# Order of products in the first projection, of casts in the down projection, and of one weight pair among the residual's quarters

## The chip, the core and the metric

The kernel runs on one core of a Trainium2 chip. The metric is the device time of one execution in microseconds (us), as a median over several runs. Engines are called PE (TensorE, matmuls), DVE (VectorE), ACT (ScalarE), POOL (GpSimd) and SP (SyncE, which issues most transfers). Each engine works through its own instructions in a fixed order and waits where an operand or a buffer is not ready.

## The reference

One block of a hybrid encoder on 256 tokens and 2048 channels in float32:

```python
hn = rmsnorm(h, mix_norm_pre)
proj = hn @ w_in                     # z, xbc, dt, u
y_ssd = ssd_mixer(z, xbc, dt, ...)   # two-directional scan, 16 heads
y_pool = pool_mixer(u, ...)
h = h + rmsnorm(concat(y_ssd, y_pool) @ w_out, mix_norm_post)
hn = rmsnorm(h, ffn_norm_pre)
gate, val = split(hn @ w_ffn_up)     # 2 x 5632 columns
ff = (gelu(conv(gate)) * val) @ w_ffn_down
h = h + rmsnorm(ff, ffn_norm_post)
gate = sigmoid(rmsnorm(h, ple_norm_pre) @ w_ple_gate)
h = h + rmsnorm(gate * (p @ w_ple), ple_norm_post)
```

## The kernel before

**Products.** A float32 product is made of three products of a shorter type. `split` (its ACT cast is L153, its DVE subtraction L154) turns a piece of weights, once its raw data have landed, into a high half (name ending in h) and a low half (ending in l, the source less the high half). `put` (L190 on ACT, L191 on DVE) does the same for activations. For each piece PE then multiplies high by high (`q == 0` in the code), and the two mixed products: `q == 1` uses the low weights, `q == 2` the low activations. All matmuls go through `mm` (L90). There are 3 buffers of raw weights, 5 each of high and low halves, 2 of the down projection's activations (`hs`), six PSUM banks called main and two called misc. Except in the up stage, where the order is written out, the order of each engine's instructions comes from the scheduler of the framework, which works from the order of the program, dependences and buffers.

**Stages on PE**, in order of time: dtu (the columns of the input projection that give dt and u), xbc, z, the scan and wo (output projection), up (gate and value columns), down, ple (second half) with the residual, gate, and the last norm.

**dtu.** The loop takes 16 tiles of 128 rows of `w_dtu` with 1056 columns each, and treats these as three thirds of 352 columns; for each of the two token halves t there are three thirds and three products, 18 matmuls per tile. The first tile is cast in three pieces, the second in pieces of 704 and 352 columns, all later ones whole. The tile of k is needed with its normalised inputs `hn(k)` (hnh, hnl in the trace). While the last tiles run, ACT reads the whole of x twice for the row norms (`rxj`, L404), builds operands for the scan, and casts the first weights of xbc (`xb_0h`, `xb_1h`); then ACT and DVE copy dtu's six banks out (`u`, L531 to L534, and `dt`, L530), and a small transpose `rxbp` on PE follows. The xbc matmuls use banks that these copies free.

**down.** 44 tiles of the hidden size, in 22 pairs (u from 0 to 21), for each half of the output columns (halves 0 and 1, main loop of `sublayer`). A pair in the list `dn_fast` goes through `seven_products`, which combines blocks (names dn..a, b, c, d, sums dns and hd) and needs fewer matmuls; a pair outside the list is a plain pair of `token_major` with whole weights (`dn_0h`, `dn_1h` and their low halves, raw tile `dn1r`). `get(k)` returns the activations of a tile and, at first use, makes them with `hid_split` (ACT cast L937, DVE subtraction L938, tile `hs`). Plain pairs between pairs of `dn_fast` are u = 6 in half 0 and u = 6, 10 and 17 in half 1; in the trace dn134 is that of u = 17, dn140 and dn142 are the last two pairs, which are plain too, and stand at the end of the list of tiles in half 1.

**Residual and gate.** Behind the last sum of down, the loop over four quarters c in `sublayer` adds the normed result to the residual (`hb`, L858), transposes that quarter on PE (`panel_part`, L391) and puts it as `dnxh` and `dnxl`. The gate matmuls (`gt`) of the quarters that are ready fill PE in between; their first weight pair (`gtf`, loaded early by `first`) is ready long before, the next pairs (`gt02`, `gt04`, `gt01` and so on; `gt_0h` and `gt_0l` in the trace, raw tile `gt0r`) are split as the gate loop comes to them. The second half of ple is copied out of its banks by ACT (`pl`, L869).

Of the kernel before, what the change touches and what calls it, by code (L numbers as in the profile page):

```python
# [53 lines left out]
def build(nc, a, out):  # L54
# [6 lines left out]
    with tile.TileContext(nc) as tc, \  # L61
# [27 lines left out]
        def mm(o, lhsT, rhs, start, stop):  # L89
            last["pe"] = ins(nc.tensor.matmul(o, lhsT, rhs, start=start, stop=stop, skip_group_check=True))  # L90
# [51 lines left out]
        def split(name, src, nel, cuts=()):  # L142

            if name in ready:
                return ready.pop(name)
            if name in spare:
                hi, lo = spare.pop(name)
            else:
                hi = wp.tile([P, 1056], F32R, tag="whi", bufs=5, name=f"{name}h")
                lo = wp.tile([P, 1056], F32R, tag="wlo", bufs=5, name=f"{name}l")  # L150
            for c0, c1 in zip((0, *cuts), (*cuts, nel)):
                s = slice(c0, c1)
                last["act"] = ins(nc.scalar.copy(hi[:, s], src[:, s]))  # L153
                last["dve"] = ins(nc.vector.tensor_sub(lo[:, s], src[:, s], hi[:, s].bitcast(F32)))  # L154
            return hi, lo
# [31 lines left out]
        def put(dst, src, scale):  # L187
# [3 lines left out]
                    ins(nc.vector.scalar_tensor_tensor(lo, src, scale, hi.bitcast(F32),  # L191
                                                       op0=ALU.mult, op1=ALU.subtract)))

        work = []

        chain = {}
# [108 lines left out]
        def token_major(name, w, c0, ks, get, acc, tail=1, fast=(), alt=None, sums=None, at=()):  # L305


            group, nu = [], len(ks) // 2
            for u in range(nu):
                if u in at:  # L310
                    at[u]()
                k0 = ks[2 * u]
                if u in fast:
                    if u == fast[0]:
                        alt = alt + [misc(f"{name}s{i}") for i in (2, 3)]
                    seven_products(f"{name}{k0}", name[:2], w, k0, c0, sums(k0), acc, alt, u == fast[0], u == fast[-1])
                    continue
                r = None if f"{name}{k0}_0" in ready else raw(f"{name}r{k0}", w[c0 // 1024, k0 // 2])
                for j in range(2):
                    group.append((k0 + j, *split(f"{name}{k0}_{j}", r and r[:, j * 1024:(j + 1) * 1024], 1024)))  # L320
                if nu - tail <= u < nu - 1:
                    continue

                order = [(t, o, g, q) for t in range(2) for o in columns(acc[t]) for g in group for q in range(3)] \
                    if u == nu - 1 or u - 1 in fast[-1:] else \
                    [(t, o, g, q) for g in group for t in range(2) for q in range(3) for o in columns(acc[t])]
                for t, (o, c), (k, wh, wl), q in order:
                    xh, xl = (v[:, t * P:(t + 1) * P] for v in get(k))
                    xx, ww = ((xh, wh), (xh, wl), (xl, wh))[q]
                    c = (c + 512 * (k + 1)) % 1024  # L330
                    mm(o, xx, ww[:, c:c + o.shape[-1]], k == ks[0] and q == 0, k == ks[-1] and q == 2)
                if u - 1 in fast[-1:]:
                    combine(name, acc, alt, nu - tail == u + 1 and tail > 1)
                group = []
                aside()
            if nu in at:
                at[nu]()
# [116 lines left out]
        for u in range(0, NK, 2):  # L454
            r = [wp.tile([P, 2048], F32, tag="raw", bufs=3, name=f"dtur{u}") if u else r0, page(f"dtur{u + 1}")]
            for j in range(2):
                k = u + j
                if k == 0:
                    last["dma"] = load(r[0][:, 704:1056], w_dtu[0][:, 704:1056])
                    xload(1, 2)  # L460
                    x_panel(1, 2)
                    continue
                for c0, c1 in ((0, 704), (704, 1056)) if k == 1 else ((0, 1056),):
                    last["dma"] = load(r[j][:, c0:c1], w_dtu[k][:, c0:c1])
                if k == 1:
                    xload(2, 4)
                elif k in (3, 5, 7):
                    xload(*{3: (4, 9), 5: (9, 13), 7: (13, 16)}[k])
                elif k == 4:
                    load(vt, a["columns"][:, :V_N - V_SCW])  # L470
                elif k == 6:
                    load(small, a["columns"][:, V_N - V_SCW:])
            if u:
                x_panel(u, u + 2)
            for j in range(2):
                k = u + j
                with tc.issue_after(front[0]), tc.issue_after(front[1]):
                    wh, wl = split(f"dtu{k}", r[j][:, :1056], 1056, ((352, 704), (704,))[k] if k < 2 else ())
                if k == 8:
                    half = last["act"], last["dve"]  # L480

                def part(t, q, ns=range(3)):
                    xh, xl = (v[:, t * P:(t + 1) * P] for v in hn(k))
                    xx, ww = ((xh, wh), (xh, wl), (xl, wh))[q]
                    for n in ns:
                        o = acc2[t][:, :352] if n == 2 else acc[t][n][:, :352]
                        mm(o, xx, ww[:, n * 352:(n + 1) * 352], k == 0 and q == 0, k == NK - 1 and q == 2)


                for a_ in ([(t, q, (n,)) for n in range(3) for q in (0, 2, 1) for t in range(2)] if k == 0 else  # L490
                           [(t, q) for t in range(2) for q in range(3)]):
                    part(*a_)

        with tc.issue_after(half[0]), tc.issue_after(half[1]):
# [293 lines left out]
        def gload(name, src):  # L788
            g = cp.tile([P, D], F32, tag="gain", name=name)
            load(g, src.partition_broadcast(P))  # L790
            return g
# [34 lines left out]
                return dict(self.got[k], a11=(h1[:, :P], l1[:, :P]), a12=(h2[:, :P], l2[:, :P]),  # L826
                            a22=(h2[:, P:], l2[:, P:]))

        def sublayer(name, w, ks, get, gain, h, vnext, panel=Panel, fast=((), ()), sums=None, at=(), row=None):

            mg = [page(f"{name}m{t}") for t in range(2)]
            sq = [[], []]
# [22 lines left out]
            for c in range(4):  # L855
                s = slice(c * 512, (c + 1) * 512)
                for t in range(2):
                    nc.vector.scalar_tensor_tensor(h[t][:, s], mg[t][:, s], r[t], h[t][:, s],  # L858
                                                   op0=ALU.mult, op1=ALU.add)
                panel_part(f"{name}x", pan, h, vnext, 4 * c, 4 * c + 4)  # L860
            return pan

        def ple(half):
# [219 lines left out]
        def first():  # L1083
# [3 lines left out]
            for j in range(2):  # L1087
                c = slice(j * 1024, (j + 1) * 1024)
                spare[f"gt00_{j}"] = hi[:, c], lo[:, c]
                ready[f"gt00_{j}"] = split(f"gt00_{j}", r[:, c], 1024)  # L1090

        hp = sublayer("dn", w_down, list(range(NF)), hid_get, gload("gffn", a["ffn_norm_post"][0]), h, V_PN,
                      fast=dn_fast, sums=hid_sums, at={11: first, NF // 2: lambda: (ple_parts(), back())}, row=rf)


        pl = [page("plb")]
# [154 lines left out]
```

## Time and profile before

| what | value |
|---|---|
| runs | 1116.56, 1115.88 and 1116.61 us, median 1116.56 |
| the profiled execution's own time | 1116.13 us |
| its span | 1114.4 us |
| granted TensorE clock | 0.998 |
| stages on PE (us from the span's start) | dtu 4.7 to 52.1, xbc to 141, z to 197, wo to 290, up to 786, down to 1009, residual and ple to 1026, gate to 1105 |

The profile is that of one execution. Its rows give a start, a duration, the engine, the line, the operation, and the tiles in the form output<-inputs with a number of instructions; in brackets stands how long the engine was idle before it, and what ended the idle time. A row of the timeline can hold several equal instructions in a row, and tile names are printed without their numbers, so that `dn_0h` stands for each plain pair's. A PE matmul is drawn longer than it keeps PE from the next one, since matmuls overlap; so distances between starts tell its cost.

### The profile page before, as it was taken

To read this page: it belongs to the slowest core of one execution; us is meant where nothing else is said; L and a number is where in the kernel's file an instruction comes from. 1 tells how busy PE (TensorE), PEld (TensorE's weight loads), DVE (VectorE), ACT (ScalarE), POOL (GpSimd) and SP (SyncE) were. 2 spreads that over 40 slices of the span, in tenths; PEclk is the share of its full clock that TensorE was granted. 3 is DMA by queue.
4 is the path that set the end of the run, shared out by engine and by line. 5 is a ranking of instruction groups with operands and counts; after the bars stand their busy time and mean duration, and the time that the engine had idled before them with its cause. 6 is when DMAs were issued, how large, how long until landed. Compare 5 with 4: busy or idle time off the path is not lost.

```text
span 1114.4 us, 16061 instructions
## 1 busy us (share of the span) xinstructions
PE 1104.0 (99%) x5964; PEld 950.6 (85%) x5964; DVE 959.6 (86%) x1338; ACT 723.8 (65%) x1056; POOL 69.0 (6%) x140
## 2 busy tenths in 40 slices
PE   9999999999999999999999999999999999999997
PEld 9999988888888888888888888888888888877876
DVE  6568997899868998888888888888899999989895
ACT  6858763555775565664655655657689878767673
POOL 0200000100100000000000000000000000001001
PEclk9999999999999999999999999999999999999999
DMA  9753346454589999999899999999999899995662
GB/s 363 314 204 137 117 188 263 151 189 178 195 343 397 382 396 385 361 378 374 335 378 385 356 377 366 352 393 391 362 382 381 322 348 403 415 378 222 265 235 105
DMA packets 54943, 347.29 MB, mean 312 GB/s; under 512 B 6096, under 2 KB 6992, under 8 KB 20176
## 3 DMA queue, kind: packets, MB, share of 16 engines
q1 hardware_dynamic: 44064, 289.53, 66.8%
q0 software_dynamic: 10368, 56.10, 13.3%
q8 instruction: 47, 0.77, 0.3%
q10 hardware_dynamic: 432, 0.62, 0.2%
q14 instruction: 32, 0.26, 0.1%
HBM read 297.48 MB, written 48.76 MB: 311 GB/s over the span
## 4 chain that ended last, share of the span: by engine, by line
PE 94%; DVE 2%; ACT 2%; issue 1%; POOL 1%; DMA 0%; SPq 0%; POOLq 0%; ACTq 0%
PE ga L90 22%; PE va L90 22%; PE dna L90 12%; PE woa L90 7%; PE xbc L90 5%; PE gt L90 5%; PE z L90 4%; PE dns L90 4%; PE dtu L90 4%; PE dn0s L90 2%; PE dn1s L90 2%; PE yd L90 1%; PE pw L90 1%; PE gts L90 1%; PE ple L90 1%
## 5 line engine op out<-in xcount | busy, mean ns | idle before, releaser
L90 PE MATMUL ga<-wox,ug_0h 128*128 128x512 f32 x352 | 125.5, 395 | 0.0
L90 PE MATMUL ga<-wox,ug_1h 128*128 128x512 f32 x352 | 125.1, 394 | 0.0
L90 PE MATMUL va<-wox,uv_1h 128*128 128x512 f32 x352 | 124.8, 393 | 0.0
L90 PE MATMUL va<-wox,uv_0h 128*128 128x512 f32 x352 | 124.8, 393 | 0.0
L90 PE MATMUL ga<-wox,ug_1l 128*128 128x256 f32 x352 | 99.1, 282 | 0.0
L90 PE MATMUL va<-wox,uv_1l 128*128 128x256 f32 x352 | 99.1, 281 | 0.0
L90 PE MATMUL va<-wox,uv_0l 128*128 128x256 f32 x352 | 99.1, 281 | 0.0
L90 PE MATMUL ga<-wox,ug_0l 128*128 128x256 f32 x352 | 99.0, 281 | 0.0
L253 DVE TENSOR_TENSOR dnb<-dnb 128x512 f32<-128x512 f32 x128 | 88.3, 690 | 3.1
L90 PEld LDWEIGHTS va<-wox,uv_1h 128*128 128x128 f32 x352 | 66.1, 188 | 15.0
L90 PEld LDWEIGHTS ga<-wox,ug_1h 128*128 128x128 f32 x352 | 66.1, 188 | 15.0
L90 PEld LDWEIGHTS va<-wox,uv_0h 128*128 128x128 f32 x352 | 66.1, 188 | 15.0
L90 PEld LDWEIGHTS ga<-wox,ug_0h 128*128 128x128 f32 x352 | 66.1, 188 | 14.9
L90 PEld LDWEIGHTS ga<-wox,ug_0l 128*128 128x128 f32 x352 | 66.2, 188 | 0.1
L90 PEld LDWEIGHTS ga<-wox,ug_1l 128*128 128x128 f32 x352 | 66.2, 188 | 0.0
L90 PEld LDWEIGHTS va<-wox,uv_0l 128*128 128x128 f32 x352 | 66.2, 188 | 0.0
L90 PEld LDWEIGHTS va<-wox,uv_1l 128*128 128x128 f32 x352 | 66.2, 188 | 0.0
L937 ACT CAST hs<-hid 128x512 fp32r<-128x512 f32 x44 | 27.3, 621 | 21.8 <-PE dna L90 21.6
L244 POOL DMA_DIRECT2D dns<-dnb x30 | 16.2, 541 | 310.9 <-DVE dnb L253 310.9
L938 DVE TENSOR_TENSOR hs<-hid,hs 128x512 fp32r<-128x512 f32 x44 | 30.2, 686 | 5.8 <-ACT hs L937 5.8
L801 ACT CAST he<-he 128x512 fp32r<-128x512 f32 x13 | 8.1, 621 | 37.7 <-DVE he L800 37.7
L90 PE MATMUL dna<-dn_1h,hs 128*128 128x512 f32 x96 | 30.9, 393 | 0.0
(2247 smaller groups left out, 3227.7 us busy)
## 6 DMA issues: line engine op xcount, KB each, us to landing
dnb<-w_down SPq DMA_DIRECT2D x32, 1024.0 KB, 9.8
dns<-dnb POOLq DMA_DIRECT2D x30, 1024.0 KB, 6.6
hd<-hsum POOLq DMA_DIRECT2D x24, 512.0 KB, 8.3
zr<-w_z SPq DMA_DIRECT2D x8, 1024.0 KB, 4.9
dtur<-w_dtu SPq DMA_DIRECT2D x14, 528.0 KB, 8.6
wo0r<-w_out_ SPq DMA_DIRECT2D x7, 1024.0 KB, 4.9
dn1r<-w_down SPq DMA_DIRECT2D x7, 1024.0 KB, 6.8
hsum<-he POOLq DMA_DIRECT2D x13, 512.0 KB, 7.7
```

The lines of the kernel that those rows point to most:

```text
L90: last["pe"] = ins(nc.tensor.matmul(o, lhsT, rhs, start=start, stop=stop, skip_group_check=True))
L244: nc.gpsimd.dma_start(t, pg[0])
L253: nc.vector.tensor_add(v[:, i], v[:, i], v[:, j])
L801: nc.scalar.copy(o[:, :512], s[:, :512])
L937: nc.scalar.copy(t[:, :512], hid_part(k))
L938: nc.vector.tensor_sub(t[:, 512:], hid_part(k), t[:, :512].bitcast(F32))
```

## The change

It has three parts.

1. In dtu the order of the products of a tile is changed. The first tile keeps its order. In the second and third, for each third of the columns, both tokens' products with high weights come first, and then all products with the low weights. In tiles 3 to 13 both tokens' high-weight products come before the low-weight ones, and in the last two tiles each token half has its low-weight product last. The stop flag of the last tile moves to the product that now comes last. The third tile's weights are cast and subtracted in two pieces, of 352 and 704 columns. No matmul is added or removed.
2. In `token_major` a plain pair that stands between two pairs of the list `fast` calls `get(k0)` directly after the pair's weight splits, ordered behind the pair's last ACT cast (`issue_after`). In down this holds for u = 6 of half 0 and u = 6, 10 and 17 of half 1. In wo `get` only returns slices, and gate has no such pair.
3. `sublayer` takes a dictionary `then` of functions to be called behind the quarters of the residual. In down's call, the function `second` loads and splits the two pieces of gate's second weight pair (`gt02`) there, one behind quarter 1 and one behind quarter 2; the gate loop then finds them in `ready`.

In the built program the changes of order are local. In dtu DVE and ACT have one more instruction each. At the border to xbc the first bank's u copies are spread otherwise over ACT and DVE, so that xbc's first bank is freed by a DVE copy of u (and by ACT's cast `xb_0h`), and its second by an ACT copy. The activations of the four plain pairs stand behind the weights' casts on ACT. On DVE, the last two pairs' low halves of weights stand ahead of sums of the banks, and `gt02`'s first low half stands between the first and second pair of the first quarter's `dnxl`, ahead of the residual's third quarter, its second low half ahead of the fourth. On PE five matmuls of `gt02` stand ahead of the third quarter's transposes, and four more gate matmuls ahead of `gt01`'s first ones. On SP one load (`plb`) stands behind a load of gate weights where it stood ahead of it; POOL's order is the same.

```diff
--- before.py
+++ after.py
@@ -191,6 +191,7 @@
                     ins(nc.vector.scalar_tensor_tensor(lo, src, scale, hi.bitcast(F32),
                                                        op0=ALU.mult, op1=ALU.subtract)))
 
+        LOW_LAST = (0, 2), (1,)
         work = []
 
         chain = {}
@@ -320,6 +321,9 @@
                     group.append((k0 + j, *split(f"{name}{k0}_{j}", r and r[:, j * 1024:(j + 1) * 1024], 1024)))
                 if nu - tail <= u < nu - 1:
                     continue
+                if fast and fast[0] < u < fast[-1]:
+                    with tc.issue_after(last["act"]):
+                        get(k0)
 
                 order = [(t, o, g, q) for t in range(2) for o in columns(acc[t]) for g in group for q in range(3)] \
                     if u == nu - 1 or u - 1 in fast[-1:] else \
@@ -475,7 +479,7 @@
             for j in range(2):
                 k = u + j
                 with tc.issue_after(front[0]), tc.issue_after(front[1]):
-                    wh, wl = split(f"dtu{k}", r[j][:, :1056], 1056, ((352, 704), (704,))[k] if k < 2 else ())
+                    wh, wl = split(f"dtu{k}", r[j][:, :1056], 1056, ((352, 704), (704,), (352,))[k] if k < 3 else ())
                 if k == 8:
                     half = last["act"], last["dve"]
 
@@ -484,11 +488,13 @@
                     xx, ww = ((xh, wh), (xh, wl), (xl, wh))[q]
                     for n in ns:
                         o = acc2[t][:, :352] if n == 2 else acc[t][n][:, :352]
-                        mm(o, xx, ww[:, n * 352:(n + 1) * 352], k == 0 and q == 0, k == NK - 1 and q == 2)
+                        mm(o, xx, ww[:, n * 352:(n + 1) * 352], k == 0 and q == 0, k == NK - 1 and q == 1)
 
 
                 for a_ in ([(t, q, (n,)) for n in range(3) for q in (0, 2, 1) for t in range(2)] if k == 0 else
-                           [(t, q) for t in range(2) for q in range(3)]):
+                           [(t, q, (n,)) for qs in LOW_LAST for n in range(3) for q in qs for t in range(2)] if k < 3 else
+                           [(t, q) for t in range(2) for q in (0, 2, 1)] if k > NK - 3 else
+                           [(t, q) for qs in LOW_LAST for t in range(2) for q in qs]):
                     part(*a_)
 
         with tc.issue_after(half[0]), tc.issue_after(half[1]):
@@ -826,7 +832,7 @@
                 return dict(self.got[k], a11=(h1[:, :P], l1[:, :P]), a12=(h2[:, :P], l2[:, :P]),
                             a22=(h2[:, P:], l2[:, P:]))
 
-        def sublayer(name, w, ks, get, gain, h, vnext, panel=Panel, fast=((), ()), sums=None, at=(), row=None):
+        def sublayer(name, w, ks, get, gain, h, vnext, panel=Panel, fast=((), ()), sums=None, at=(), row=None, then=()):
 
             mg = [page(f"{name}m{t}") for t in range(2)]
             sq = [[], []]
@@ -858,6 +864,8 @@
                     nc.vector.scalar_tensor_tensor(h[t][:, s], mg[t][:, s], r[t], h[t][:, s],
                                                    op0=ALU.mult, op1=ALU.add)
                 panel_part(f"{name}x", pan, h, vnext, 4 * c, 4 * c + 4)
+                if c in then:
+                    then[c]()
             return pan
 
         def ple(half):
@@ -1089,8 +1097,13 @@
                 spare[f"gt00_{j}"] = hi[:, c], lo[:, c]
                 ready[f"gt00_{j}"] = split(f"gt00_{j}", r[:, c], 1024)
 
+        def second(j):
+            if j == 0:
+                cur["gt"] = raw("gt0r2", w_gate[0, 1])
+            ready[f"gt02_{j}"] = split(f"gt02_{j}", cur["gt"][:, j * 1024:(j + 1) * 1024], 1024)
+
         hp = sublayer("dn", w_down, list(range(NF)), hid_get, gload("gffn", a["ffn_norm_post"][0]), h, V_PN,
-                      fast=dn_fast, sums=hid_sums, at={11: first, NF // 2: lambda: (ple_parts(), back())}, row=rf)
+                      fast=dn_fast, sums=hid_sums, at={11: first, NF // 2: lambda: (ple_parts(), back())}, row=rf, then={1: lambda: second(0), 2: lambda: second(1)})
 
 
         pl = [page("plb")]
```

## The prediction

> **What bounds the kernel now.** I read the busy line first, then the table of TensorE's (PE's) waits, then PE's timeline at the places which the change touches, and last the engine that releases each wait there.
>
> ```profile
> PE 1104.0 (99%) x5964; PEld 950.6 (85%) x5964; DVE 959.6 (86%) x1338; ACT 723.8 (65%) x1056; POOL 69.0 (6%) x140
> ```
>
> PE works for 1104.0 of 1114.4 us, so nearly all of the time is matmul work, and the change takes no matmul away. Only time in which PE stands or crawls can be won. The waits that the table names at the places of the change are small:
>
> ```profile
> PE gt L90 <- DVE gt_0l L154: 0.8, 1, 0.8
> ...
> PE dna L90 <- ACT dn_0h L153: 0.3, 1, 0.3
> ```
>
> The columns are the waiting tile, its releaser, the total, the count and the longest. No row names the up stage, which runs from 290 to 786 us; what is won before it therefore passes through it as an earlier start. The table undercounts, because a matmul whose operand comes late is partly drawn as a longer matmul. I therefore measure each loss as a distance between starts, less the number of matmuls times their pitch. Two stretches of the table by windows serve below (busy time and instructions by engine, then clock, DMA share, GB/s):
>
> ```profile
> 907.50:981.00 73.50, 73.50 (x320) 59.81 (x319) 69.86 (x86) 60.06 (x75) 6.13 (x11) 1.00 1.00 400
> ...
> 1012.00:1026.40 14.40, 13.55 (x75) 10.71 (x74) 14.07 (x24) 10.86 (x21) 0.21 (x1) 1.00 0.68 273
> ```
>
> The first gives the pitch of a 512-column matmul: 73.50 / 320 = 0.230 us.
>
> **Part A, dtu (edits to its order, its third tile and its stop flag).** The rows are PE's starts, with durations and counts.
>
> ```profile
> 7.84 0.81 PE L90 MATMUL dtu<-dtu1h,hnh 128*128 128x352 f32 x3
> ...
> 11.38 0.64 PE L90 MATMUL dtu<-dtu2h,hnh 128*128 128x352 f32 x3
> ...
> 14.47 0.65 PE L90 MATMUL dtu<-dtu3h,hnh 128*128 128x352 f32 x3
> ...
> 52.10 0.61 PE L90 MATMUL rxbp<-ident,rxbw 128*128 128x128 f32 x4
> ...
> 52.66 0.39 PE L90 MATMUL xbc<-hnh,xb_0h 128*128 128x256 f32 x1
> ```
>
> From 14.47 to 52.10 there are 13 tiles of 18 matmuls: 37.63 / 234 = 0.161 us each. From 7.84 to 14.47 there are 36, worth 5.79, but they take 6.63: 0.84 is lost in the second and third tile, where the low half of the weights comes late. The change puts products with low weights last in a tile. When are they there?
>
> ```profile
> 7.01 1.17 ACT L153 CAST dtu1h<-dtur 128x704 fp32r<-128x704 f32 x2 [0.84 <-DMA dtur<-w_dtu]
> ...
> 9.51 1.08 ACT L153 CAST dtu2h<-dtur 128x1056 fp32r<-128x1056 f32 x1 [0.43 <-DMA dtur<-w_dtu]
> ```
> ```profile
> 7.82 1.33 DVE L154 TENSOR_TENSOR dtu1l<-dtur,dtu1h 128x704 fp32r<-128x704 f32 x2 [1.06 <-ACT dtu1h L153]
> ...
> 10.62 1.26 DVE L154 TENSOR_TENSOR dtu2l<-dtur,dtu2h 128x1056 fp32r<-128x1056 f32 x1 [0.68 <-ACT dtu2h L153]
> ```
>
> Second tile: twelve high products run from 7.84 to 9.77. Its two low pieces are ready by 9.15 (DVE, from 7.82 on, 1.33), so the six low ones run to 10.73. The third tile's high cast starts at 9.51. Cut in two it costs more; the second tile has the same two widths already (minimum and maximum of its row are 352 and 704 columns):
>
> ```profile
> L153 ACT CAST dtu1h<-dtur x2: 482/632/781, 7.0 to 7.7; 128x704 fp32r<-128x704 f32 x1, 128x352 fp32r<-128x352 f32 x1
> ```
>
> The pair takes ACT 1.17 against 1.08 for the whole, and DVE 1.33 against 1.26: 0.09 and 0.07 more. The first piece is cast by 9.99, the second by about 10.7, and they are needed from 10.73 and 11.38 on; the low pieces follow one DVE piece (about 0.9) behind, near 11.7, and are needed at 10.73 + 12 × 0.161 = 12.66. So the extra 0.16 lies under PE's second tile, and the fourth tile starts at 10.73 + 18 × 0.161 = 13.62 instead of 14.47. If this cover were gone, the price is that 0.16.
>
> [...]
>
> All later tiles have their operands early (no wait in the table), so dtu would end at 51.25, 0.85 early. What is late next is the border to xbc. Its first matmul needs the cast xb_0h, and its bank the copies of dtu's results (u).
>
> ```profile
> 27.57 1.27 SPq L120 DMA_DIRECT2D x<-x  x2
> ...
> DMA to landing us min/median/max: 7.3/8.4/9.5
> ```
> ```profile
> 34.91 1.07 ACT L153 CAST dtu14h<-dtur 128x1056 fp32r<-128x1056 f32 x1 [1.79 <-PE dtu L90]
> ...
> 35.88 1.91 ACT L404 ACTIVATE rxj<-x 128x2048 f32<-128x2048 f32 x1
> ...
> 50.16 1.05 ACT L153 CAST xb_0h<-xb2r 128x1024 fp32r<-128x1024 f32 x1
> ```
> ```profile
> 51.24 1.23 DVE L154 TENSOR_TENSOR xb_0l<-xb2r,xb_0h 128x1024 fp32r<-128x1024 f32 x1 [0.26 <-ACT xb_0h L153]
> ...
> 52.55 0.58 DVE L532 TENSOR_SCALAR u<-dtu,rx0r 128x352 f32<-128x352 f32 x1
> ```
>
> The ACT row of 34.91 waited for PE, so it moves up by 0.85. The row behind it reads x, whose first half was issued at 27.57 and landed after the minimum of 7.3, thus at 34.9: it can move from 35.88 to about 34.9. From there ACT is a chain without gaps to xb_0h at 50.16, which comes near 49.2. In the changed program the first u pair needed at the border comes partly on ACT behind two xb casts and partly on DVE behind xb_0l (51.24, 1.23): DVE ends its u at about 52.15 instead of 52.55 + 0.58, and xbc starts near 52.2 instead of 52.66. I take **0.46 gained**. Ends: 0.85 if the border passes everything, and −0.5 if the ACT chain does not move and xbc waits for copies that stand behind the casts (start at 53.15). I choose by the DVE rows, which are nearest. The stop flag costs nothing: the last product is only another one.
>
> **Part B, activations behind weights (plain pairs between pairs of seven products).** Four pairs change: one in half 0, three in half 1. In the last of them:
>
> ```profile
> 981.11 0.39 PE L90 MATMUL dn1s<-dn132ch,hd 128*128 128x512 f32 x1
> ...
> 983.61 0.62 PE L90 MATMUL dna<-dn_0h,hs 128*128 128x512 f32 x2
> ```
> ```profile
> 975.32 0.62 ACT L937 CAST hs<-hid 128x512 fp32r<-128x512 f32 x1 [1.57 <-PE dna L90]
> ...
> 980.16 0.62 ACT L937 CAST hs<-hid 128x512 fp32r<-128x512 f32 x1 [2.32 <-PE dna L90]
> ...
> 980.68 1.04 ACT L153 CAST dn_0h<-dn1r 128x1024 fp32r<-128x1024 f32 x1
> ```
> ```profile
> 981.76 1.23 DVE L154 TENSOR_TENSOR dn_0l<-dn1r,dn_0h 128x1024 fp32r<-128x1024 f32 x1 [0.25 <-ACT dn_0h L153]
> ```
>
> The cast at 980.16 is of the pair after this one: it waits on ACT for a buffer that PE frees, dn_0h, the weights that PE needs next, stands queued behind it, and dn_0l on DVE behind that. From 981.11 to 983.61 are 7 matmuls; at 0.230 they need 1.61 and take 2.50: **0.89** lost.
>
> In the changed program ACT casts dn_0h and dn_1h first, then this pair's activations (the cast that sat at 975.32), then the next pair's. ACT idled 2.32 before 980.16, thus from 977.84, and one cast fewer (0.5 to 0.62) stands ahead: dn_0h runs from about 977.3, dn_1h to 979.4 (1.04 each), the activations to 980.0; their buffer was free at 975.32, where that cast had waited for it. They are needed at 981.11 + 0.23 = 981.34: margin 1.3. On DVE, dn_0l, dn_1l and the activations' low part (1.23, 1.23 and about 0.7 from 978.6 on) end near 981.7; that part is needed seven matmuls on, at 982.95: margin 1.2. So all 0.89 is won, and what queues behind is only the next pair's cast, which waits until 980.16 in any case. At the other three places the table shows no wait, so nothing is won there; the activations come up to 2.1 later on ACT (two casts of 1.04); the margin of 1.3 at the fourth place is what remains after that delay, so I take the loss at nothing. What it costs if that cover is gone stands in rival 4. Who waits behind the activations' cast on ACT now is only the next pair's weights. Ends: 0.89 gained, or nothing where the wait passes from the weights to the activations (rival 3).
>
> The last two pairs' order changes too, because the weights' low half is subtracted earlier:
>
> ```profile
> 998.12 0.50 PE L90 MATMUL dna<-dn_0l,hs 128*128 128x512 f32 x1
> ...
> 1003.09 0.85 PE L90 MATMUL dna<-dn_0h,hs 128*128 128x512 f32 x3
> ...
> 1004.71 0.39 PE L90 MATMUL dna<-dn_0h,hs 128*128 128x512 f32 x1
> ```
> ```profile
> 1003.11 1.21 DVE L154 TENSOR_TENSOR dn_0l<-dn1r,dn_0h 128x1024 fp32r<-128x1024 f32 x1
> ```
>
> From 1003.09 to 1004.71 are 6 matmuls: 1.62 against 1.38, 0.24 lost, behind a low half that DVE only started at 1003.11; and the matmul at 998.12 takes 0.50 where its neighbours take 0.39, about 0.12 lost. In the changed program both low halves stand about 1 us earlier in DVE's queue, ahead of the sums of the banks. **0.36 gained**; ends 0 and 0.36, and I take the upper one since 1 us exceeds both losses. What then waits are the bank sums (0.69 each), which no matmul needs for 3 us.
>
> **Part C, gate's second weight pair among the residual's quarters.**
>
> ```profile
> 1019.03 0.63 PE L90 MATMUL gt<-gt_0h,dnxh 128*128 128x512 f32 x2
> ...
> 1020.51 0.73 PE L90 MATMUL gt<-gt_0l,dnxh 128*128 128x512 f32 x2 [0.85 <-DVE gt_0l L154]
> ...
> 1021.31 1.03 PE L391 MATMUL dnxt<-ident,hb 128*128 128x128 f32 x8
> ...
> 1023.40 0.50 PE L90 MATMUL gt<-gtfh,dnxh 128*128 128x512 f32 x1
> ```
> ```profile
> 1019.25 1.21 DVE L154 TENSOR_TENSOR gt_0l<-gt0r,gt_0h 128x1024 fp32r<-128x1024 f32 x1
> ```
>
> From 1019.03, two matmuls (0.46) should bring the next at 1019.49; it comes at 1020.51: 1.02 lost on gt_0l, which DVE began at 1019.25. Its raw data and its high half are there (the matmuls at 1019.03 use them). Changed, DVE subtracts it behind the first quarter's first pair, at about 1015.0 to 1016.2, and the second half near 1020.2, needed at 1020.87: margin 0.6. The moves cost no instruction: the same two casts, two subtractions and one load, which passes nothing in SP's queue but one later load. DVE has no room to spare: in 1012 to 1026.4 it is busy for 14.07 of 14.40, so the two subtractions (2.4 together) push the residual's last two quarters back: the last is done near 1022.3 instead of 1018.5. Of these, the third quarter's transposes ran at 1021.31, and nine matmuls of gate now run ahead of them and of the bank below, so they are covered. What is late next is a bank:
>
> ```profile
> 1022.76 0.59 ACT L869 ACTIVATE pl<-ple 128x512 f32<-128x512 f32 x1
> ```
>
> The matmul at 1023.40 needs the bank that ACT's copy frees at 1022.76 + 0.59 = 1023.35. Before, that cost 0.06; now PE comes about 1 us sooner and stands 0.36, but with four more matmuls behind it (0.92). I take **0.92 gained**; ends 0 (the bank takes all) and 1.02.
>
> **The sum.** 0.46 + 0.89 + 0.36 + 0.92 = 2.63. Later waits follow PE's own progress and keep their size. The profiled execution took 1116.13, its span 1114.4 and 1.7 around it; 1116.13 − 2.63 = 1113.5. The median of the runs shown is 1116.56, 0.43 above that execution, so the median forecast is **1113.9**.
>
> **The rivals.**
> (1) The border swallows part A: ACT's chain does not move, for x lands later, and the start of xbc goes to 53.15. For it: x's second landing is 9.5. Against it: the chain's start needs the first half alone. 0.46 becomes −0.5: 1114.9.
> (2) Part C is given back at the bank or by DVE's pace: 2.63 − 0.92, thus 1114.9. For it: DVE's 14.07 of 14.40, the margin of 0.6. Against: the four matmuls that are moved ahead have their operands.
> (3) Part B doesn't do what it says: the wait passes from the weights to the activations, and 0.89 is gone: 1114.8. For it: five operations now end within 1.3 of their use. Against: their buffer is free 4 us ahead.
> (4) Slower: the casts behind which the activations now stand wait for a late weight transfer.
>
> ```profile
> 966.19 0.33 SPq L120 DMA_DIRECT2D dn1r<-w_down  x1
> ...
> DMA to landing us min/median/max: 4.7/6.8/11.4
> ```
>
> In 907.5 to 981 the DMA share is 1.00. Before, a late pair cost PE only the wait for its own cast; now dn_1h and the activations' cast come in one row behind that, 1.04 + 0.62 = 1.66 more. It decides from a landing past about 977.3 − 966.19 + 1.3 = 12.4 us; the row's maximum is 11.4 and its median 6.8.
>
> [...]
>
> At two of the four places: 3.3 lost, with B's 0.89 gone, 1116.56 − 1.74 + 3.3 = 1118.1.
>
> **How the numbers follow.** Forecast 0.62, rivals (1) 0.13, (2) 0.11, (3) 0.08, (4) 0.06. About 0.2%, 2.2 us, is what a measurement of this kernel can tell from no change, so the border lies at 1114.3: the forecast is faster, (1) to (3) are the same, (4) is slower. Faster 0.62, same 0.32, slower 0.06. The low end: every part at its upper end is 0.85 + 0.89 + 0.36 + 1.02 = 3.12, 1113.4, and the shown runs spread by 0.7 downwards: 1112.8. The high end takes in two rivals together, (1) and (2) (gain 0.74, 1115.8), less a little as both at full are rare: 1115.6.
>
> **What would show it.** A: the second and third tile without stretched starts, the fourth at 13.6, dtu's end at 51.25, xbc's start near 52.2. B: the matmuls at 981 at pitch, ACT's dn_0h there near 977.3. The pairs before 1005 at pitch. C: no wait on gt_0l, a wait of about 0.4 at the bank. The prediction is wrong if xbc starts at 52.66 or later, if the activations' cast is what PE waits for at any plain pair, or if a new wait appears on the up stage's raw loads.

## The result, and the profile after

| kernel | runs | median us | range |
|---|---|---|---|
| before | 10 | 1116.22 | 1115.74 to 1116.61 |
| changed | 10 | 1113.45 | 1113.06 to 1114.04 |

The ratio is 0.9975, with a 95% interval of 0.9968 to 0.9983: 2.77 us less. The profiled execution of the changed kernel took 1113.60 us with a span of 1111.8; that of before took 1116.13 and 1114.4. So the two traces differ by 2.5 to 2.6, and they can be laid side by side. First the busy line of the changed kernel, and one row of its table of PE's waits (waiting tile, releaser, total, count, longest):

```profile
PE 1102.2 (99%) x5964; PEld 951.3 (86%) x5964; DVE 959.5 (86%) x1339; ACT 724.0 (65%) x1057; POOL 75.7 (7%) x140
```
```profile
PE xbc L90 <- DVE u L538: 0.4, 1, 0.4
```

Of the two waits shown before, on gt_0l and on dn_0h, the table has neither any more; the one on u at the start of xbc is new. PE is busy for 1102.2 instead of 1104.0 although it runs the same 5964 matmuls: part of the lost time was drawn as long matmuls.

Where the time came from is read by laying the starts of the stages beside each other. PE's timeline, before (z, down, gate, and the last norm's matmuls):

```profile
140.95 0.63 PE L90 MATMUL z<-z_0h,hnh 128*128 128x512 f32 x2
...
786.11 0.62 PE L90 MATMUL dna<-dn_0h,hs 128*128 128x512 f32 x2
...
1015.40 0.62 PE L90 MATMUL gt<-gtfh,dnxh 128*128 128x512 f32 x2
...
1105.15 1.02 PE L90 MATMUL gof<-hb,ident 128*128 128x512 f32 x2
```

and changed:

```profile
140.73 0.63 PE L90 MATMUL z<-z_0h,hnh 128*128 128x512 f32 x2
...
785.85 0.62 PE L90 MATMUL dna<-dn_0h,hs 128*128 128x512 f32 x2
...
1013.82 0.62 PE L90 MATMUL gt<-gtfh,dnxh 128*128 128x512 f32 x2
...
1102.65 1.02 PE L90 MATMUL gof<-hb,ident 128*128 128x512 f32 x2
```

The lead is 0.22 at z, 0.26 at down, 1.58 at gate and 2.50 at the end. So dtu gave about 0.2 in this pair of traces, down 1.32 and gate 0.92.

**dtu and the border.** PE's starts in the changed kernel:

```profile
8.00 0.59 PE L90 MATMUL dtu<-dtu1h,hnh 128*128 128x352 f32 x2
...
10.03 1.12 PE L90 MATMUL dtu<-dtu1l,hnh 128*128 128x352 f32 x6
...
10.99 0.48 PE L90 MATMUL dtu<-dtu2h,hnh 128*128 128x352 f32 x2
...
13.89 0.65 PE L90 MATMUL dtu<-dtu3h,hnh 128*128 128x352 f32 x3
...
51.53 0.60 PE L90 MATMUL rxbp<-ident,rxbw 128*128 128x128 f32 x4
...
52.50 0.36 PE L90 MATMUL xbc<-hnh,xb_0h 128*128 128x256 f32 x1 [0.37 <-DVE u L538]
```

From 8.00 to 13.89 the second and third tile take 5.89 instead of 6.63, a saving of 0.74. The six matmuls with low weights stand in one row (10.03), and the third tile follows 0.96 behind, at pitch. But the second tile began 0.16 later than before, and xbc starts 0.97 after the small transposes at 51.53 instead of 0.56. What it waited for is seen on ACT and DVE:

```profile
33.39 1.08 ACT L153 CAST dtu14h<-dtur 128x1056 fp32r<-128x1056 f32 x1 [1.59 <-PE dtu L90]
...
35.16 1.92 ACT L408 ACTIVATE rxj<-x 128x2048 f32<-128x2048 f32 x1 [0.69 <-DMA x<-x]
```
```profile
50.48 1.22 DVE L154 TENSOR_TENSOR xb_0l<-xb2r,xb_0h 128x1024 fp32r<-128x1024 f32 x1 [0.26 <-ACT xb_0h L153]
...
51.78 0.57 DVE L538 TENSOR_SCALAR u<-dtu,rx0r 128x352 f32<-128x352 f32 x1
```

ACT had cast dtu14 by 34.47 and then stood 0.69 until x had landed. DVE makes u only behind xb_0l, and xb_0l hangs on ACT's chain behind x.

**The pair of u = 17 in down.**

```profile
980.84 0.39 PE L90 MATMUL dn1s<-dn132ch,hd 128*128 128x512 f32 x1
...
981.06 0.63 PE L90 MATMUL dna<-dn_0h,hs 128*128 128x512 f32 x2
...
981.53 0.63 PE L90 MATMUL dna<-dn_0l,hs 128*128 128x512 f32 x2
...
982.46 0.39 PE L90 MATMUL dna<-dn_0l,hs 128*128 128x512 f32 x1
```
```profile
976.65 1.05 ACT L153 CAST dn_0h<-dn1r 128x1024 fp32r<-128x1024 f32 x1
...
978.56 0.61 ACT L945 CAST hs<-hid 128x512 fp32r<-128x512 f32 x1
...
979.89 0.62 ACT L945 CAST hs<-hid 128x512 fp32r<-128x512 f32 x1 [0.71 <-PE dna L90]
```

From 980.84 to 982.46 there are 7 matmuls in 1.62: pitch. ACT cast dn_0h at 976.65 and this pair's activations at 978.56; the cast that waits for its buffer (979.89, the next pair's activations) has only later weights behind it.

**The last two pairs.** PE's last matmul ahead of them and its first one behind them, and DVE's low half for the last pair:

```profile
996.04 0.39 PE L90 MATMUL dn1s<-dn138ch,hd 128*128 128x512 f32 x1
...
1007.40 0.39 PE L90 MATMUL ple<-ple_0h,pth 128*128 128x512 f32 x1
```
```profile
999.87 1.22 DVE L154 TENSOR_TENSOR dn_0l<-dn1r,dn_0h 128x1024 fp32r<-128x1024 f32 x1
```

Between these two starts are 49 matmuls in 11.36, 0.232 each, and no distance between two of them stands out. The low half that DVE started at 1003.11 before starts at 999.87.

**Gate.** The table by windows (the stretch, then busy time and instruction count of PE, PEld, DVE, ACT, POOL, clock, DMA share, GB/s):

```profile
1012.00:1026.40 14.40, 14.28 (x77) 11.74 (x76) 13.66 (x22) 12.19 (x23) 0.46 (x1) 1.00 0.63 239
```

In 1012 to 1026.4 PE is busy for 14.28 instead of 13.55, with DVE at 13.66 of 14.40.

```profile
1017.44 0.62 PE L90 MATMUL gt<-gt_0h,dnxh 128*128 128x512 f32 x2
...
1017.89 0.62 PE L90 MATMUL gt<-gt_0l,dnxh 128*128 128x512 f32 x2
...
1021.08 0.63 PE L90 MATMUL gt<-gt_0h,dnxh 128*128 128x512 f32 x2
...
1021.83 0.50 PE L90 MATMUL gt<-gtfh,dnxh 128*128 128x512 f32 x1
```
```profile
1021.18 0.59 ACT L877 ACTIVATE pl<-ple 128x512 f32<-128x512 f32 x1
```

The matmuls with gt_0l follow at pitch (1017.44, 1017.89). Ahead of 1021.83 two matmuls of 0.23 started at 1021.08, so the next could start at 1021.54: 0.29 is lost at the bank that ACT's copy frees at 1021.18 + 0.59 = 1021.77.

### The profile page after: what moved, and what is told of

It is laid out like the page before. It is cut to its first block, busy times and chain, and to the rows that moved or that the text cites. A ratio compares the mean times of both kernels' runs of the same rounds, so it can differ in the third digit from the quotient of the medians.

```text
span 1111.8 us, 16068 instructions
## 1 busy us (share of the span) xinstructions
PE 1102.2 (99%) x5964; PEld 951.3 (86%) x5964; DVE 959.5 (86%) x1339; ACT 724.0 (65%) x1057; POOL 75.7 (7%) x140
## 4 chain that ended last, share of the span: by engine, by line
PE 92%; ACT 3%; DMA 2%; DVE 1%; issue 1%; POOL 0%; SPq 0%; POOLq 0%; ACTq 0%
PE ga L90 22%; PE va L90 22%; PE dna L90 12%; PE woa L90 7%; PE xbc L90 5%; PE gt L90 5%; PE z L90 4%; PE dns L90 4%; PE dn0s L90 2%; PE dn1s L90 2%; DMA dtur<-w_dtu 2%; PE ple L90 1%; DMA x<-x 1%; PE yd L90 1%; PE pw L90 1%
## 5 line engine op out<-in xcount | busy, mean ns | idle before, releaser
L90 PE MATMUL dna<-dn_0h,hs 128*128 128x512 f32 x96 | 31.3, 394 | 0.0
```

## Experiments

They come in three groups, each with runs of the kernel before beside it, whose medians were 1116.29, 1116.33 and 1116.29. The first group takes the change apart.

**Part 1, dtu, alone.** Only the hunks of the diff in the dtu loop:

```diff
-    wh, wl = split(f"dtu{k}", r[j][:, :1056], 1056, ((352, 704), (704,))[k] if k < 2 else ())
+    wh, wl = split(f"dtu{k}", r[j][:, :1056], 1056, ((352, 704), (704,), (352,))[k] if k < 3 else ())
...
+    [(t, q) for qs in LOW_LAST for t in range(2) for q in qs]):
```

> The kernel before with the change in dtu alone. Theory (the border limits it): in the changed kernel 36 matmuls of the second and third tile took 5.89 us instead of 6.63, but xbc waited 0.37 for DVE's copy u behind xb_0l, so 0.3 of the 0.74 is left. Alone: fourth tile 0.7 to 0.8 closer to the second tile's start, from the second tile's start to xbc's first matmul 0.2 to 0.5 less than the 44.82 of before, time 0.2 to 0.5 below the kernel before. Rival (the saving passes whole when the down and gate parts are not there): 0.75 less. Rival (nothing passes): 0.0.

It took 1115.82 (ratio 0.9996, interval 0.9987 to 1.0005), 0.47 less than before; within the noise, in the expected direction. Its trace is sharper than the time. PE:

```profile
8.27 0.48 PE L90 MATMUL dtu<-dtu1h,hnh 128*128 128x352 f32 x2
...
14.03 0.65 PE L90 MATMUL dtu<-dtu3h,hnh 128*128 128x352 f32 x3
...
52.31 0.36 PE L90 MATMUL xbc<-hnh,xb_0h 128*128 128x256 f32 x1
```

From 8.27 to 14.03 are 5.76 (before 6.63), and from 8.27 to 52.31 are 44.04 instead of 44.82: 0.78. That is the upper rival's figure, yet the mechanism is the theory's. In this run PE's first tile was late (its last third began at 7.31, where before had 6.72), so the second began at 8.27, where before had 7.84; ACT read x at 34.97, 0.37 after it could have, and xbc started at 52.31, only 0.35 ahead of before. A border that is set by x does not move with the second tile; the distance from that tile's start, which the expectation used, was the wrong measure.

**Part 2, down, alone.**

```diff
+                if fast and fast[0] < u < fast[-1]:
+                    with tc.issue_after(last["act"]):
+                        get(k0)
```

> The kernel before with the change in the plain pairs of down alone. Theory: the 7 matmuls at the pair of u = 17 run at pitch, 0.88 won there, and about 0.4 at the last two pairs, since the order of the last two pairs comes with this part; gate still waits 1.0 for gt_0l. Time 1.2 to 1.3 below before. Rival (the last two pairs' gain belongs to the residual's part): 0.9. Rival (the waiting DVE work behind takes it back at the residual, since the gate still waits there for DVE): 0.4.

It took 1114.85 (0.9987, 0.9978 to 0.9996), 1.44 less. From the last matmul of the pair before dn134 to gate's first one it needs 32.97 us, as the changed kernel does (32.98), against 34.29 before: 1.32. Two of its waits stand at gate:

```profile
PE dnxt L394 <- DVE dnxl L191: 0.4, 1, 0.4
...
PE gt L90 <- DVE gt_0l L154: 0.4, 1, 0.4
```

Gate's low half is still late here, by 0.4 instead of 0.8, and the third quarter's transposes ahead of it wait 0.4 for dnxl. From gate's start to the last norm it takes 89.62, against 89.75 before and 88.83 changed. So part 2 carries the last two pairs' gain and gives nothing back; 0.13 more of it falls in gate, which the expectation (1.2 to 1.3) had not counted.

**Part 3, gate's second weight pair, alone.**

```diff
+        def second(j):
+            if j == 0:
+                cur["gt"] = raw("gt0r2", w_gate[0, 1])
+            ready[f"gt02_{j}"] = split(f"gt02_{j}", cur["gt"][:, j * 1024:(j + 1) * 1024], 1024)
...
-    at={...}, row=rf)
+    at={...}, row=rf, then={1: lambda: second(0), 2: lambda: second(1)})
```

> The kernel before with gate's second weight pair amid the residual's quarters alone. Theory: no wait on gt_0l (1.02 won), a wait of 0.3 at ple's bank in place of 0.06 less what runs ahead of it, 0.9 won in all, pair of u = 17 as before (0.9 lost there). Rival (the gain needs the earlier end of down, because the margin of gt_1l is only 0.6): a wait on gt_1l of 0.3 to 0.6 appears, 0.3 to 0.6 won. Rival (bank takes all): 0.0 to 0.2.

It took 1115.16 (0.999, 0.9981 to 0.9999), 1.13 less. PE:

```profile
1015.80 0.63 PE L90 MATMUL gt<-gtfh,dnxh 128*128 128x512 f32 x2
...
1019.43 0.61 PE L90 MATMUL gt<-gt_0h,dnxh 128*128 128x512 f32 x2
...
1019.88 0.62 PE L90 MATMUL gt<-gt_0l,dnxh 128*128 128x512 f32 x2
...
1023.08 0.63 PE L90 MATMUL gt<-gt_0h,dnxh 128*128 128x512 f32 x2
1023.59 0.50 PE L90 MATMUL gt<-gtfh,dnxh 128*128 128x512 f32 x1
```

gt_0l comes at pitch behind 1019.43, and there is no wait on the second half. The two matmuls at 1023.08 reach to 1023.54, and the bank's matmul comes at 1023.59: the bank costs 0.05 here, where the expectation had 0.3. PE starts the third quarter's transposes 5.70 behind gate's first matmul, one matmul earlier in its order than in the changed kernel (5.92), and ACT's copy of ple, which comes behind these transposes, starts 7.15 behind it instead of 7.36. From gate's start to the last norm it takes 88.64, which is 1.11 less than before, where the changed kernel has 0.92 less. So the gain doesn't need the other parts; it is a little larger without them.

Alone, the three give 0.47 + 1.44 + 1.13 = 3.04, together 2.77. The traces have the difference in gate: part 2 alone saves 0.13 there and part 3 alone 1.11, the two in one kernel 0.92, which is 0.32 less. This is not scatter between executions: from gate's start to the last norm it takes 88.82 to 88.85 in all seven traces of kernels with the changed gate as it is.

**Third tile in one piece.**

```diff
-    ((352, 704), (704,), (352,))[k] if k < 3 else ())
+    ((352, 704), (704,))[k] if k < 2 else ())
```

> The changed kernel with the third tile of dtu cast in one piece, as before. Theory: with the low weights last the whole cast is soon enough (cast from 9.60 for 1.08, so at 10.68, needed at 10.99; low part near 11.95, needed at 12.92): no loss, 0.0 against the changed kernel, 2.8 below before. Rival (the pieces carry the gain of the third tile): the third tile starts 0.2 to 0.4 late, and the time is up to 0.3 above the changed kernel.

It took 1113.58 (0.9977, 0.9967 to 0.9986), 2.71 less than before: the same as the changed kernel. ACT and PE:

```profile
9.66 1.08 ACT L153 CAST dtu2h<-dtur 128x1056 fp32r<-128x1056 f32 x1 [0.36 <-DMA dtur<-w_dtu]
```
```profile
11.04 0.48 PE L90 MATMUL dtu<-dtu2h,hnh 128*128 128x352 f32 x2
...
13.93 0.65 PE L90 MATMUL dtu<-dtu3h,hnh 128*128 128x352 f32 x3
```

The whole cast ends at 10.74, and PE takes it at 11.04; to the fourth tile it is 2.89, as at pitch (18 × 0.161 = 2.90). So the pieces bring nothing once the low weights come last. It also gave the first hint of the border: ACT read x at 34.60 and xbc started at 51.95, 17.35 behind; in the changed kernel it is 35.16 and 52.50, in part 1 alone 34.97 and 52.31, 17.34 both times. Here, however, ACT read x directly behind its cast of dtu14 (34.52, then 34.60), and PE didn't stand at the border: xbc starts 0.37 behind the small transposes, as in e6 below, where nothing holds it.

**x released earlier.**

```diff
-                if k == 8:
+                if k == 7:
                     half = last["act"], last["dve"]
```

> The changed kernel with the loads of x released behind dtu's weight tile 7 instead of tile 8. Theory (x's landing sets the border): in the runs so far xbc started 17.34 after ACT's first reading of x, whenever that was (34.60, 34.97 and 35.16 against 51.95, 52.31 and 52.50). With x there sooner ACT reads it right behind dtu14's cast, near 34.5, and xbc starts within 0.1 of the end of the small transposes behind dtu: 0.3 to 0.4 less wait, time 0.2 to 0.4 below the changed kernel. Rival (DVE's order, u behind xb_0l, whatever ACT does): the wait stays at 0.3 to 0.4. Rival (the earlier transfer takes the DMA engines from dtu's last weights): a wait for dtu weights appears, slower.

It took 1113.55 (0.9973, 0.9963 to 0.9984), as the changed kernel, and did not test what it was meant to. SP issued x at 27.86 here and at 27.95 in the changed kernel:

```profile
27.86 0.91 SPq L120 DMA_DIRECT2D x<-x  x2
```
```profile
27.95 0.91 SPq L120 DMA_DIRECT2D x<-x  x2
```

The condition that the edit loosened was not what held the transfer: on SP it stands directly behind the issues of dtu's weights, which last until 27.81 here and 27.91 there. The border fits the rule again (ACT at 35.19, xbc at 52.54: 17.35).

**u ahead of xbc's first low half on DVE.**

```diff
-        spare, ready = {}, {}
+        spare, ready, hold = {}, {}, {}
...
+                with tc.issue_after(hold[name]) if name in hold else nullcontext():
                     last["dve"] = ins(nc.vector.tensor_sub(lo[:, s], src[:, s], hi[:, s].bitcast(F32)))
...
+            u_ = ins(nc.vector.tensor_scalar(ut[:, t * 1024 + 320:t * 1024 + 672], acc[t][1][:, :352], rx[t], None,
...
+            if t == 0:
+                hold["xb20_0"] = u_
```

> The changed kernel with DVE's subtraction of xbc's first low half ordered behind its first u copy. Theory: u no longer hangs on ACT's chain behind x, so xbc's start does not wait for u; it waits at most for the low half, which is three matmuls later (0.5 on from the start, DVE done by 52.1 to 52.6). xbc's start moves to the end of the small transposes, but the third matmul waits 0 to 0.4. Against the changed kernel: 0.1 to 0.4 less. Rival (the border is bound by the low half itself): 0.0, the wait moves from u to xb_0l.

It took 1113.24 (0.9973, 0.9962 to 0.9984). DVE and PE:

```profile
49.80 0.58 DVE L539 TENSOR_SCALAR u<-dtu,rx0r 128x352 f32<-128x352 f32 x1
...
50.30 1.22 DVE L155 TENSOR_TENSOR xb_0l<-xb2r,xb_0h 128x1024 fp32r<-128x1024 f32 x1
```
```profile
51.21 0.60 PE L90 MATMUL rxbp<-ident,rxbw 128*128 128x128 f32 x4
...
51.57 0.36 PE L90 MATMUL xbc<-hnh,xb_0h 128*128 128x256 f32 x1
```

u is made at 49.80, and xbc starts at 51.57, 0.36 behind the small transposes' start, with no wait; its third matmul (the first with xb_0l) starts at 51.89 and does not wait either. x landed late here too (ACT had stood 0.46 for it, and read it at 34.60), but xbc started 16.97 behind that, so the rule of 17.34 is broken by the order on DVE alone. This settles the border: the wait was u behind xb_0l behind ACT's chain. The 0.2 by which its median is lower than the changed kernel's is within the noise of either; the wait's absence is not.

**Second half of ple placed earlier.**

```diff
-    then={1: lambda: second(0), 2: lambda: second(1)})
+    then={1: lambda: (second(0), ple1.append(ple(1))), 2: lambda: second(1)})
...
-        pl.append(ple(1))
+        pl += ple1
```

> The changed kernel with the second half of ple (its copies on ACT) placed in the program behind the residual's second quarter instead of behind all four. Theory (the bank behind ACT's copy is what is late next in gate): the copies come ahead of gt04's casts, gate's second column half has its banks before 1018, no bank wait there (0.3 of the changed kernel's), but ACT's casts of gt04 come 2.2 later: 0.2 to 0.3 less than the changed kernel if these have margin. Rival (ACT or DVE is the bound in this stretch): a wait on gt04's halves of 0.3 or more appears and the time is the same or up to 0.5 above.

It took 1113.24 (0.9971, 0.996 to 0.9983). ACT and PE:

```profile
1012.94 1.08 ACT L877 ACTIVATE pl<-ple 128x512 f32<-128x512 f32 x2
```
```profile
1017.59 0.62 PE L90 MATMUL gt<-gtfh,dnxh 128*128 128x512 f32 x2
...
1018.04 0.61 PE L90 MATMUL gt<-gtfl,dnxh 128*128 128x512 f32 x2
```

ACT's copies come 8 us earlier, gate's second column half fills PE from 1017.59 on at pitch, and no bank wait is left. From gate's start to the last norm it takes 88.43 instead of 88.83: 0.40. This is the bank's 0.29, and 0.11 more whose place isn't shown.

**The new place of the activations at u = 17 alone.**

```diff
-                if fast and fast[0] < u < fast[-1]:
+                if name == "dn1" and u == 17:
```

> The changed kernel with the activations behind the weights at u = 17 of half 1 alone; at the three other places in the old order. Theory (the other places gave nothing): same as the changed kernel, within 0.15. Rival (they gave the part of down's gain that the pair of u = 17 and the last two pairs don't explain): 0.2 to 0.4 above the changed kernel. Rival (they cost something under cover): up to 0.3 below it.

It took 1113.41 (0.9974, 0.9964 to 0.9984): the same as the changed kernel. The other three places neither gave nor cost anything that the time can show.

**The changed kernel again, the two improvements together, and the order of two tiles.**

> The changed kernel itself, beside the two below and on the same chip. Theory: 2.6 to 3.0 below before, xbc waits for u 0.2 to 0.5 (xbc's start 17.34 behind ACT's first reading of x), bank wait of 0.3 in gate. It gives the reference for the other two.

It took 1113.45 (0.9976, 0.9967 to 0.9985), xbc 17.35 behind ACT's first reading of x (34.97, 52.32).

The next kernel holds the edits of e6 and e7 at once.

> The changed kernel with u ahead of xbc's first low half on DVE and the second half of ple placed behind the residual's second quarter. Theory (each removes a wait of its own, 0.37 at the border and 0.29 at the bank): 0.4 to 0.7 below the changed kernel, 3.2 to 3.5 below before. Rival (a later wait takes one of the two back): 0.1 to 0.3 below the changed kernel.

It took 1112.89 (1112.43 to 1113.25; ratio 0.9971, 0.9959 to 0.9982), 3.40 less than before, and 0.56 less than the changed kernel in the same group. Neither wait is in its trace, and its lead over the changed kernel's run of the group is 0.58 at z (139.97 against 140.55) and 1.02 at the last norm (1101.49 against 1102.51). Of the 1.02, a part is that the profile took its fastest execution (1112.43). It is the fastest of these kernels; the intervals of the two ratios overlap, so its advantage rests on the two waits that are gone from the trace and on ranges that barely touch.

```diff
-                        mm(o, xx, ww[:, n * 352:(n + 1) * 352], k == 0 and q == 0, k == NK - 1 and q == 1)
+                        mm(o, xx, ww[:, n * 352:(n + 1) * 352], k == 0 and q == 0, k == NK - 1 and q == 2)
...
-                           [(t, q) for t in range(2) for q in (0, 2, 1)] if k > NK - 3 else
-                           [(t, q) for qs in LOW_LAST for t in range(2) for q in qs]):
+                           [(t, q) for t in range(2) for q in range(3)]):
```

> The changed kernel with the new order of products in the second and third tile of dtu alone, tiles 3 to 15 in the old order. Theory (later tiles have their weights early): same as the changed kernel within 0.15, fourth tile at the same distance from the second tile's start (5.8 to 5.9). Rival (the order of the middle or the last tiles carries a part): 0.2 or more above it, with stretched starts in the tiles from the fourth on or a later border.

It took 1113.33 (0.9974, 0.9965 to 0.9983): the same. PE:

```profile
8.78 0.48 PE L90 MATMUL dtu<-dtu1h,hnh 128*128 128x352 f32 x2
...
14.55 0.65 PE L90 MATMUL dtu<-dtu3h,hnh 128*128 128x352 f32 x3
```

5.77 from the second tile to the fourth. The new order of the tiles from the fourth on brings nothing that a time can show. In the traces it does something. From the fourth tile's start to ACT's cast of dtu14, which waits for PE, it is 20.44 here and before, and 19.50 in the changed kernel; and xbc starts 0.57 behind the small transposes here and 0.56 before, but 0.37 in e4 and e7, where x was on time.

## Why the prediction was right, point by point

- **The time.** Forecast 1113.9 median and 2.63 gained, measured 1113.45 and 2.77. The gain lies 0.14 beside the forecast; the rest of the distance is the median of before, which in these runs was 1116.22 where the first three had given 1116.56.
- **Part A.** The loss of 0.84 and its removal were right: 5.76 to 5.89 for the 36 matmuls where 5.79 was worked out. (The 0.84 is that of one trace: in the two others without part 1 the same matmuls took 6.56 and 6.26, so 0.77 and 0.47 were lost.) The cover over the third tile's two pieces was there (the two casts took 1.18 and ended at 10.78, PE began the tile at 10.99), and e4 shows that the pieces were not needed. The border was named as what is late next, with the right chain: x, ACT, xb_0h, u. Two steps inside it were off, in opposite directions. ACT's cast of dtu14 was taken to move up by 0.85 and moved up by 1.52 (34.91 to 33.39): 0.58 came from the fourth tile's earlier start, and 0.94 from the new order of the later tiles, which the prediction took to change nothing. And x was taken to land at 34.9, from its issue at 27.57 before; issued at 27.95, it landed at 35.16. So ACT was ready sooner and x came later. The lead at z was 0.22 in the profiled pair where 0.46 was forecast. Over the traces, xbc started at 52.66, 53.11 and 53.08 in the three kernels without part 1, and between 51.95 and 52.55 in seven with it whose border was otherwise left as in the change (e11, with the old order of the later tiles, 52.75): means 52.95 and 52.33, 0.6 apart, of which 0.14 is that the second tile began that much earlier in the seven. The term's mechanism was right; that its size fits so well is in part luck, for it depends on when x lands. The price of rival 1 (a start at 53.15) did not appear.

How far it depends on x can be read from nine traces, those with the new order in dtu's last tiles. For each, this table has how long after the start of dtu14's cast ACT read x, and how long after the start of the small transposes xbc began (us):

| kernel | x read | xbc begun |
|---|---|---|
| changed | 1.77 | 0.97 |
| e1, part 1 alone | 1.45 | 0.64 |
| e4, third tile whole | 1.16 | 0.37 |
| e5, x's condition loosened | 1.92 | 1.12 |
| e7, ple earlier | 1.18 | 0.37 |
| e8, u = 17 alone | 1.45 | 0.67 |
| e9, changed again | 1.84 | 1.05 |
| e6, u ahead of xb_0l | 1.53 | 0.36 |
| e10, u and ple | 1.54 | 0.36 |

In the first seven the second figure is 0.78 to 0.81 less than the first: what x is late passes whole to xbc. In e4 and e7 x is on time (read 0.08 and 0.10 behind the end of that cast), and nothing is left of the wait; there xbc starts 43.91 and 43.79 behind the second tile's start, against 44.82 before. In the last two, with u ahead on DVE, a late x no longer matters.

- **Part B.** 0.89 was forecast at the pair of u = 17, and it is 0.88 (7 matmuls at pitch; the lead grows from 0.27 at 980.84 to 1.15). dn_0h came at 976.65 where about 977.3 was worked out, since the casts for the pair ahead of it (dn132) had stood behind this pair's activations too and also moved up (dn132dh from 975.84 to 973.89). The last two pairs run at pitch, as forecast, and that came with this part (e2): from 1.15 at their start to 1.58 at gate's start the lead grows by 0.43, where 0.36 was forecast. That makes 1.32 in all against 1.25. Rival 3 (the wait passes to the activations) is out: they were ready at 979.17 and needed at 981.06. Rival 4 had no late transfer to start from: at none of the four pairs did ACT's casts wait for their weights in this trace (dn_0h begins at 811.67, 921.74, 941.82 and 976.65, with no wait drawn).
- **Part C.** Forecast 0.92, measured 0.92 (1.58 to 2.50). The step at the bank was forecast too: 0.36 of wait, and 0.29 came, at 1021.83. Part 3 alone gives 1.11, so the forecast's price is that of the parts together. The margin of 0.6 on the second half held; PE did not wait there.
- **The sum.** The parts were taken as independent. Part 1 is: its lead of 0.22 at z is still 0.26 at down, 645 us later, and between the two the tables of PE's waits name none that would take it away. Parts 2 and 3 are nearly so: in gate they give 0.32 less together than the sum of what each gives there alone, and this accounts for the 0.27 between the parts' sum (3.04) and the whole (2.77).

What stays open: whether x can be issued earlier, since e5 did not move it, and why the built order puts the third quarter's transposes one matmul earlier when part 3 stands alone.

## What to carry to other kernels

When PE is 99% busy, measure a loss as the distance between starts less the matmuls at pitch; the table of waits showed 0.3 where 0.89 was lost. A cast that waits for a buffer should not stand in a queue ahead of casts whose data are there; ordering it behind them gave 0.88 of the 0.89 back without one instruction less. When a start is always the same distance behind some earlier event (here 17.34 behind x's first reading), that is a hint and not yet a proof: e4 and e7 have the same distance, though PE did not wait in them. What shows that the event sets the start is that its lateness comes out again in full, and that one change of order between the two breaks the link. And parts that are worth 3.04 one by one can be worth 2.77 together; the stage in which they meet shows where the rest went.

## What was not expected of the hardware

dtu's second tile began between 7.81 and 8.78 in thirteen profiled executions, of kernels that start alike. Two things are seen there. In before and in the changed kernel ACT's cast of that tile stood 0.84 and 0.93 for the raw weights and began at 7.01 and 7.16; in part 2 alone, where the second tile began at 8.36, PE stood 0.43 for that cast. In the three latest starts (8.63, 8.76 and 8.78, in e3, e7 and e11) the tables of PE's waits name no wait for it, and it is PE's first tile that is late: its middle third began at 6.62, 6.64 and 6.63, against 5.76 in before and 5.82 in the changed kernel, while the granted clock of these three executions was 0.998, 0.998 and 0.997. Why it was late stays open.

Where a late x holds the border, a later beginning costs nothing: e1 began 0.40 later than e9 and reached xbc at 52.31, e9 at 52.32. Where x is on time, it is carried on: e7 began 0.72 later than e4 and reached xbc 0.60 later. With starts that differ so, a difference of under 1 us between two single traces says nothing here before their starts are compared.
